# A two-layer encoder: the second attention layer's transposes go from TensorE to VectorE and memory, its loads are split by use, its heads queue in line

## The chip, the cores and the metric

The kernel runs on one core of a Trainium2 chip. The metric is the device time of one execution in microseconds (us), lower is better. Engines are named as in the profile: PE is TensorE (matmuls and transposes), PEld its weight load, DVE VectorE, ACT ScalarE, POOL GpSimd, SP SyncE (it issues loads). ACTq and SPq are the queues in which ACT and SP issue transfers.

## The reference

All tensors are float32; x is 256 tokens by 2048. Cut to what matters here:

```python
for i in range(2):
    hn = rms_norm(h, attn_norm[i])
    # i = 0: windowed attention, 32 heads of 64 in 4 key groups, sink logit
    # i = 1: differential attention, 8 heads of 2 x 128
    h = h + (windowed_gqa_sink, diff_attention)[i](hn, ...)
    h = h + swiglu(rms_norm(h, ffn_norm[i]), w_ffn_in[i], w_ffn_out[i])   # hidden width 5632
    gate = sigmoid(rms_norm(h, ple_gate_norm[i]) @ ple_w_gate[i])
    h = h + rms_norm(p[i] @ ple_w_proj[i], ple_post_norm[i]) * gate

def diff_attention(...):                  # the layer that the change is mostly about
    qkv = h @ w_qkv                       # 2048 x 6144
    q, k = rms_norm(q, q_gain), rms_norm(k, k_gain)    # per head, two maps of 128 each
    sc = q @ k.T * scale - slope * dist   # for each head and each of its two maps
    probs = softmax(sc)
    wts = probs[0] - lam * probs[1]
    o = rms_norm(wts @ v, subln) * (1 - lambda_init)   # 256 columns a head
    return o @ w_o
```

## The kernel before, in words

Every product with a weight matrix is a list of *groups*. A group makes a strip of 512 output columns for all 256 tokens: up to 16 k-tiles of 128 rows, two row tiles of 128 tokens, and three matmuls each (activation low x weight high, high x high, high x low, in a reduced float32 format), so 96 matmuls of width 512 for a full group (L177, `mm<-ws,xt`). There are 9600 of them. The high and low parts of a weight block of two k-tiles come from `split_block`: ACT casts (L139), DVE subtracts (L140). Raw blocks of 1 MB are loaded through SP's queue into three buffers, and split blocks of two k-tiles live in four. `split` and `split_scaled` do the same for activations (ACT L207 or L211, then DVE L208 or L212).

The order in which the code emits instructions is set by `Flow`, a clock that exists only while the program is built. Each wide matmul advances it by `MM = 0.23`; `later(delay, fn)` puts a piece of other work on a heap, and after each matmul at most one step of the earliest due piece is emitted. A piece written as a generator emits one step per `yield` (0.1 on the clock, or the value yielded). If a group needs an operand that isn't there yet, `flow.until` empties the heap ahead of time ("forced"), and the pieces then stand in PE's order back to back. PE follows this order throughout; ACT and DVE follow their written order in the first group only, and are ordered by the compiler's scheduler afterwards.

The matmul contracts over partitions, so activations must be turned before they are used. There are two ways. One is PE transposes of 128x128 through PSUM (L306, L441, L483, L700, L807). The other is `turned`, a *trip through memory*: DVE transposes in blocks of 32x32 (L266), ACT issues one write to DRAM (L268), after 3.0 on the clock four reads that put the blocks in place (L273), and after another 5.0 the consumer's splits. Before, only the feed-forward's hidden values and the residual strips take trips, with a buffer for the write and another for the read.

The stages in order: the first attention layer (`AttentionA`: groups of keys and values, then four of queries), its output projection in parts of 8, 4 and 4 k-tiles, feed-forward and gate, the second attention layer (`AttentionB`), its projection in parts of 8 and 8, feed-forward and gate. The attention pieces are threaded into the groups by `Flow`.

In `AttentionB` a strip of two heads has a group of queries, one of keys, one of values. After a group of queries or keys, `qk_norm` squares (ACT L414), sums (DVE), makes reciprocal roots on POOL (up to L418), and scales the result to `qn` (DVE L430). Then `to_pairs` turns each head by four PE transposes (L441) and splits it. Scores (L449, six matmuls a map) and `exps` (DVE L463 and L466, ACT L469) follow; POOL and DVE combine the two maps, `keys_first` turns the weights by four PE transposes (L483), `weigh` multiplies them with the values (L677, 12 matmuls), the output is normed and `out` turns it by four PE transposes (L700).

In `AttentionA` the same steps run for 16 pairs of heads (scores L449, weights turned at L483, keys at L528, products with values L588). Its buffers are counted in `busy`: a piece whose buffers are taken tries again each 0.6 on the clock (`when`).

At the start x comes in eight pieces of 256 columns, with a weight block behind each second one (`load_x`, `feed.fetch`), and `put_x` turns and splits two pieces at a time.

Of the kernel before, what the change touches and what calls it, by code (L numbers as in the profile page):

```python
# [12 lines left out]
F32 = mybir.dt.float32  # L13
# [72 lines left out]
def encoder(ctx: ExitStack, tc: tile.TileContext, x, p, attn_norm, ffn_norm, a_w_qkv, a_q_norm,  # L86
# [171 lines left out]
    def turned(srcs, then):  # L258


        (tag0, tag1), ap = spare[0], spare[1]
        both = [ap.tile([P, 2, 2, T], F32R, name=t, tag=t, bufs=n).bitcast(F32).rearrange("p a b t -> p (a b t)")
                for t, n in (tag0, tag1)]
        st = both[0].rearrange("p (f t m) -> p f m t", m=NM, t=32)
        for m in range(NM):
            nc.vector.transpose(out=st[:, :, m, :], in_=srcs[m].rearrange("p (f t) -> p f t", t=32))  # L266
        d = dram.tile([P, 2 * W], F32, name="sq32")
        nc.scalar.dma_start(out=d, in_=both[0])  # L268

        def read():  # L270
            for b in range(4):
                r = slice(32 * b, 32 * b + 32)
                nc.scalar.dma_start(out=both[1][r].rearrange("f (k g i) -> f k g i", k=SK, g=4),  # L273
                                  in_=d.rearrange("(g f) (k b i) -> b f k g i", g=4, k=SK, b=4)[b])
            flow.later(5.0, lambda: then(both[1].rearrange("f (k t m) -> f k m t", k=SK, m=NM)))
        flow.later(3.0, read)
# [86 lines left out]
    def put_x(q):  # L363

        if q == 0:
# [31 lines left out]
    spare = [None, None]  # L397

    def phase(name, tags):

        phases.close()
        spare[:] = tags, phases.enter_context(tc.tile_pool(name=name, bufs=1, reuse_waits="tile"))
        return spare[1]
# [72 lines left out]
    busy = {"e": 0, "wT": 0, "q": 0}  # L476
# [12 lines left out]
    def when(kind, limit, take, fn):  # L489

        def piece():
            if busy[kind] + take > limit:
                flow.later(0.6, piece)
            else:
                busy[kind] += take
                return fn()
        return piece

    class AttentionA:
        def __init__(self, norm):  # L500
            self.norm, self.os, self.kd, self.vp = norm, Slots(), [], []
            self.ap = phase("attn0", (("wT", WT_BUFS), ("wT", WT_BUFS)))
# [33 lines left out]
        def queries(self, s):  # L536
            def then(toks):
                for b in range(2):
                    flow.later(5.0 + 8.0 * b, when("q", 2, 1, lambda b=b: self.to_q(2 * s + b, toks, b)))
# [5 lines left out]
        def to_q(self, qg, toks, b):  # L545
# [3 lines left out]
            for i in range(2):  # L549
                flow.later(2.0 + 8.6 * i, when("e", E_BUFS, 2, lambda i=i: self.heads(qg * 2 + i, qT, left)))  # L550

        def heads(self, j, qT, left):
# [8 lines left out]
            if not left:  # L561
                busy["q"] -= 1
# [8 lines left out]
            flow.later(10.0, when("wT", WT_BUFS, 2, lambda: self.turn(j, es)))  # L571

        def turn(self, j, es):
            wts = []
            for e in es:
                yield from keys_first(e, self.ap, WT_BUFS, wts)
                busy["e"] -= 1
            flow.later(3.5, lambda: self.weigh(j, wts))

        def weigh(self, j, wts):  # L580
            ps = at_ps()[:, 0, :]
            n = 0
            for e2 in range(2):
                c0 = j // 4 * P + 64 * (1 - e2)
                for kh in range(2):
                    v, wT = self.vp[kh], wts[e2]
                    for a, b in ((1, 0), (0, 1), (0, 0)):
                        nc.tensor.matmul(ps, v[:, a, c0:c0 + P], wT[:, b, kh, :], start=(n == 0), stop=(n == 11))  # L588
                        n += 1
                        yield  # L590
            busy["wT"] -= 2
# [9 lines left out]
    class AttentionB:  # L601
# [3 lines left out]
        def start(self):  # L605
            self.ap = phase("attn1", (("qk0", 2), ("qk1", 2)))
# [3 lines left out]
        def side(self, s, which):  # L610
# [9 lines left out]
        def turn_side(self, hd, which, toks, b):  # L620
            s = self.hd.setdefault(hd, {"e": {}})
            t = self.ap.tile([P, 2, 2, T], F32R, name=f"qk{which}", tag=f"qk{which}", bufs=2)
# [17 lines left out]
        def scores(self, hd, c):  # L640
# [6 lines left out]
            if c == 1:  # L647
# [8 lines left out]
                flow.later(9.0, lambda: self.turn(hd, e1))  # L656

        def turn(self, hd, e):
            got = []
            yield from keys_first(e, self.ap, 2, got)  # L660
            flow.later(3.5, lambda: self.weigh_when_ready(hd, got[0]))
# [7 lines left out]
        def weigh(self, hd, wT):  # L669
# [16 lines left out]
            def scale():  # L686
                on = []
                for m in range(NM):
                    t = self.ap.tile([P, T], F32, name="on", tag="on", bufs=4)
# [3 lines left out]
                flow.later(2.5, lambda: self.out(hd, on))  # L693
            flow.later(7.0, scale)

        def out(self, hd, on):
            ps = at_ps()
            for j in range(2):
                for m in range(NM):
                    nc.tensor.transpose(ps[:, j, mslice(m)], on[m][:, j * P:(j + 1) * P], ident)  # L700
                    yield
            for j in range(2):
                o = pair()
                split_scaled(o[:, 0, :], o[:, 1, :], ps[:, j, :], subln[:, j:j + 1])
                self.os.put(2 * hd + j, halves_of(o))
# [34 lines left out]
    class FeedForward:  # L740
# [4 lines left out]
        def start(self):  # L745
            self.fp = fp = phase(f"ffn{self.layer}", (("sq32", 2), ("turned", 2)))
# [217 lines left out]
```

## Time and profile before

| | before |
|---|---|
| time, median of 3 runs | 2348.84 us (2347.53 to 2349.82) |
| time of the profiled execution | 2351.27 us |
| its span | 2349.5 us |
| mean granted clock of PE | 0.997 |
| PE busy | 2319.2 us, 99% |
| DVE, ACT, POOL busy | 1383.7, 1118.2, 146.9 us |
| moved by DMA | 459.10 MB |

The median says what a user gets; the durations of single instructions come from the one profiled execution, whose time is 2.43 us above the median. The span runs from its first to its last recorded instruction. A granted clock of 1 stands for 2.4 GHz.

### The profile page before, as it was taken

The page shows a single profiled execution, that of the slowest core. Times are in us where ns is not written, and L with a number is a line of the kernel's source. Part 1 is how long each engine was busy: PE and PEld are TensorE (multiplying, and loading weights), DVE is VectorE, ACT ScalarE, POOL GpSimd, SP SyncE. Part 2 cuts the span into 40 slices and gives each one's busy share as a digit, 9 for nine tenths or more (in the row PEclk, how much of TensorE's full clock was granted, in tenths as well). Part 3 has the DMA queues.
Part 4 walks back from the last instruction along what each step waited for, and adds up shares of the span by engine and source line. Part 5 has one row for each costly group of instructions (what it writes and reads, how often), then busy time and mean ns, then how long its engine had stood idle before and what let it go on. Part 6 is the DMA issues. An engine that isn't in the chain of part 4 may idle for free.

```text
span 2349.5 us, 28062 instructions
## 1 busy us (share of the span) xinstructions
PE 2319.2 (99%) x10525; PEld 1906.5 (81%) x10525; DVE 1383.7 (59%) x1670; ACT 1118.2 (48%) x1557; POOL 146.9 (6%) x311
## 2 busy tenths in 40 slices
PE   8999999999999999999999999999999999999999
PEld 6877778888888888878888888788888888888877
DVE  5777765545554554566666666655545555555564
ACT  5555454444433444455555545554444434444453
POOL 1342000000000000000111120000000000000000
PEclk9999999999999999999999999999999999999999
DMA  6432566556656655577645454766556556655663
GB/s 238 157 112 93 173 231 215 199 197 206 215 187 208 213 196 189 206 235 229 206 160 178 164 177 162 240 235 201 197 193 224 201 189 210 210 197 204 208 218 140
DMA packets 186992, 459.10 MB, mean 195 GB/s; under 512 B 75264, under 2 KB 78440, under 8 KB 186600
## 3 DMA queue, kind: packets, MB, share of 16 engines
q1 hardware_dynamic: 120568, 424.27, 52.1%
q10 hardware_dynamic: 66288, 33.04, 5.2%
q8 instruction: 82, 1.34, 0.2%
q14 instruction: 54, 0.44, 0.1%
HBM read 439.95 MB, written 17.30 MB: 195 GB/s over the span
## 4 chain that ended last, share of the span: by engine, by line
PE 90%; DMA 4%; DVE 2%; ACT 2%; ACTq 1%; issue 1%; POOL 0%; SPq 0%; DVEq 0%
PE mm L177 86%; DMA turned<-sq 2%; PE at L449 1%; PE at L588 1%; DVE ws L140 1%; ACT ws L139 1%; DMA qk<-sq 1%; PE at L483 1%; ACTq L273 1%; PE at L677 1%; DMA raw<-in_a_w_qkv_dram 0%; ACT xt L211 0%; PE at L441 0%; DMA sq<-qk 0%; PE at L807 0%
## 5 line engine op out<-in xcount | busy, mean ns | idle before, releaser
L177 PE MATMUL mm<-ws,xt 128*128 128x512 f32 x9600 | 2286.0, 394 | 12.5 <-DVE ws L140 7.0
L177 PEld LDWEIGHTS mm<-ws,xt 128*128 128x128 f32 x9600 | 1794.6, 188 | 408.7 <-DVE ws L140 13.3
L140 DVE TENSOR_TENSOR ws<-raw,ws 128x1024 fp32r<-128x1024 f32 x800 | 973.1, 1223 | 779.3 <-ACT ws L139 772.5
L139 ACT CAST ws<-raw 128x1024 fp32r<-128x1024 f32 x800 | 837.5, 1052 | 975.0 <-PE mm L177 904.6
L218 POOL TENSOR_SCALAR rs_v<-ssum 128x2 f32<-128x2 f32 x8 | 3.6, 448 | 1690.3 <-DVE ssum L251 1690.3
L335 DVE TENSOR_TENSOR h<-mm,h 128x512 f32<-128x512 f32 x104 | 68.6, 685 | 24.2 <-PE mm L177 24.0
L469 ACT ACTIVATE e<-e,nm 128x257 f32<-128x257 f32 (+1 forms) x96 | 47.9, 501 | 10.1 <-DVE nm L466 9.7
L588 PE MATMUL at<-wT,vp 128*128 128x256 f32 x192 | 49.3, 288 | 0.7 <-DVE wT L208 0.7
L220 POOL TENSOR_TENSOR rs_y<-rs_v,halves 128x2 f32<-128x2 f32 (+2 forms) x29 | 49.0, 1690 | 2.4
L483 PE MATMUL at<-ident,e 128*128 128x128 f32 x160 | 42.2, 272 | 0.7 <-DVE e L463 0.7
L449 PE MATMUL at<-kd,qT 128*128 128x512 f32 x96 | 36.7, 407 | 3.2 <-DVE wT L208 2.5
L779 ACT ACTIVATE silu<-mm,rinv 128x512 f32<-128x512 f32 x44 | 29.9, 688 | 19.1 <-PE mm L177 19.0
L463 DVE SCALAR_TENSOR_TENSOR e<-dist,at 128x256 f32<-128x256 f32 x96 | 36.1, 412 | 2.5 <-PE at L449 2.4
L568 POOL TENSOR_SCALAR e<-e,rd 128x256 f32<-128x256 f32 x64 | 33.1, 532 | 61.7 <-DVE rd L472 61.3
L588 PEld LDWEIGHTS at<-wT,vp 128*128 128x128 f32 x192 | 34.9, 196 | 1.8 <-ACT e L469 1.1
L247 ACT ACTIVATE sq<-h 128x512 f32<-128x512 f32 x48 | 29.9, 624 | 12.9 <-DVE h L335 4.5
L430 DVE TENSOR_TENSOR qn<-mm,rr 128x512 f32<-128x512 f32 x24 | 15.8, 685 | 31.5 <-POOL rr L418 31.5
L211 ACT ACTIVATE xt<-turned,gains 128x256 fp32r<-128x256 f32 x36 | 15.9, 514 | 36.1 <-DMA turned<-sq 36.1
L466 DVE TENSOR_REDUCE nm<-e 128x2 f32<-128x514 f32 (+1 forms) x48 | 32.2, 678 | 0.4
L207 ACT CAST xt<-turned 128x256 fp32r<-128x256 f32 x56 | 19.6, 421 | 24.7 <-DMA turned<-sq 24.7
L208 DVE TENSOR_TENSOR wT<-at,wT 128x512 fp32r<-128x512 f32 x40 | 27.0, 685 | 6.7 <-ACT wT L207 6.6
L787 DVE SCALAR_TENSOR_TENSOR hid<-mm,rinv,silu 128x512 f32<-128x512 f32 x44 | 30.9, 743 | 0.0
(109 smaller groups left out, 719.4 us busy)
## 6 DMA issues: line engine op xcount, KB each, us to landing
raw<-in_w_ffn_in_dram SPq DMA_DIRECT2D x352, 512.0 KB
raw<-in_w_ffn_out_dram SPq DMA_DIRECT2D x176, 512.0 KB
raw<-in_b_w_qkv_dram SPq DMA_DIRECT2D x96, 512.0 KB
raw<-in_ple_w_gate_dram SPq DMA_DIRECT2D x64, 512.0 KB
raw<-in_a_w_qkv_dram SPq DMA_DIRECT2D x40, 512.0 KB
raw<-in_a_w_o_dram SPq DMA_DIRECT2D x32, 512.0 KB
raw<-in_b_w_o_dram SPq DMA_DIRECT2D x32, 512.0 KB
sq<-sq ACTq DMA_DIRECT2D x23, 512.0 KB
```

The costliest lines, as they stand in the source:

```text
L139: nc.scalar.copy(out=ws[:, 0], in_=src)
L140: nc.vector.tensor_tensor(out=ws[:, 1], in0=src, in1=ws[:, 0].bitcast(F32), op=ALU.subtract)
L177: nc.tensor.matmul(ps[m], x[:, a, m], w, start=(k == 0 and i == 0), stop=(k == self.n - 1 and i == 2))
L220: nc.gpsimd.tensor_tensor(out=y, in0=v, in1=halves[:, :n], op=ALU.pow)
L335: nc.vector.tensor_tensor(out=hs, in0=ps[m], in1=hs, op=ALU.add)
L449: nc.tensor.matmul(ps[m], q[:, a, mslice(m)], k[:, b], start=(i == 0), stop=(i == 2))
L463: nc.vector.scalar_tensor_tensor(out=sc[:, m, :T], in0=d[:, m, :], scalar=-slope, in1=pss[m], op0=ALU.mult, op1=ALU.add)
L466: nc.vector.tensor_reduce(out=nm, in_=sc, axis=AX.X, op=ALU.max, negate=True)
L469: nc.scalar.activation(out=sc[:, m, :], in_=sc[:, m, :], func=AF.Exp, bias=nm[:, m:m + 1], accum_out=den[:, m:m + 1])
L483: nc.tensor.transpose(ps[:, kh, mslice(m)], w[:, m, kh * P:(kh + 1) * P], ident)
L568: nc.gpsimd.tensor_scalar(out=e[:, m, :T], in0=e[:, m, :T], scalar1=rd[:, m:m + 1], scalar2=1.0, op0=ALU.mult, op1=ALU.mult)
L588: nc.tensor.matmul(ps, v[:, a, c0:c0 + P], wT[:, b, kh, :], start=(n == 0), stop=(n == 11))
```

## The change

**Trips in the second layer.** Queries, keys, weights and outputs of `AttentionB` are no longer turned by PE. `turned` takes them on a trip, for the whole strip of two heads in the case of queries and keys (512 KB) and for one head in the case of weights and outputs (256 KB, `n=2`). The trip now writes from and reads back into one buffer instead of two.

**Loads by use.** The first weight block is loaded in halves, each behind a piece of x, and `put_x` turns one piece of x at a time with a weight split after each.

**Heads in line.** In `AttentionA` a piece that needs buffers stands in a line (`Budget`) and is started when an earlier piece gives them back, in place of trying again each 0.6; some delays are shorter, and `weigh` emits three matmuls a step.

The diff, cut to its core:

```diff
-        return [(raw, t) for t in range(0, n, 2)]
+        load_rows(raw, w, r0, n, c, slice(0, n))
+        return [(raw, t) for t in range(0, n, 2)]
+
+    def load_rows(raw, w, r0, n, c, t):
         for i in range(2):
-            nc.sync.dma_start(out=raw[:, i, :n, :],
-                              in_=w[2 * c + i, r0 * T:(r0 + n * P) * T].rearrange("(p t n) -> p t n", p=P, t=n))
+            nc.sync.dma_start(out=raw[:, i, t, :],
+                              in_=w[2 * c + i, r0 * T:(r0 + n * P) * T].rearrange("(p t n) -> p t n", p=P, t=n)[:, t])
...
-    def turned(srcs, then):
+    def turned(srcs, then, n=SK):
-        (tag0, tag1), ap = spare[0], spare[1]
-        both = [ap.tile([P, 2, 2, T], F32R, name=t, tag=t, bufs=n).bitcast(F32).rearrange("p a b t -> p (a b t)")
-                for t, n in (tag0, tag1)]
-        st = both[0].rearrange("p (f t m) -> p f m t", m=NM, t=32)
+        tag, bufs, ap = spare
+        both = ap.tile([P, 2, 2, T], F32R, name=tag, tag=tag, bufs=bufs).bitcast(F32)
+        both = both.rearrange("p a b t -> p (a b t)")[:, :n * T]
+        st = both.rearrange("p (f t m) -> p f m t", m=NM, t=32)
         for m in range(NM):
             nc.vector.transpose(out=st[:, :, m, :], in_=srcs[m].rearrange("p (f t) -> p f t", t=32))
-        d = dram.tile([P, 2 * W], F32, name="sq32")
-        nc.scalar.dma_start(out=d, in_=both[0])
+        d = dram.tile([P, n * T], F32, name=f"sq{n}", tag=f"sq{n}")
+        nc.scalar.dma_start(out=d, in_=both)
...
-    def put_x(q):
+    def put_x(i):
...
-        for i in (2 * q, 2 * q + 1):
-            yield from norm_a.turn(2 * i)
-            if i % 2 == 0:
-                feed.split()
+        yield from norm_a.turn(2 * i)
+        feed.split()
...
-    def when(kind, limit, take, fn):
...
+    class Budget:
+        def __init__(self, free):
+            self.free, self.line = free, []
+        def when(self, take, fn):
+            def piece():
+                self.line.append((take, fn))
+                self.serve()
+            return piece
+        def give(self, n):
+            self.free += n
+            self.serve()
+        def serve(self):
+            while self.line and self.line[0][0] <= self.free:
+                take, fn = self.line.pop(0)
+                self.free -= take
+                flow.later(0.0, fn)
...
-            self.ap = phase("attn0", (("wT", WT_BUFS), ("wT", WT_BUFS)))
+            self.qs, self.es, self.wts = Budget(2), Budget(E_BUFS), Budget(WT_BUFS)
+            self.ap = phase("attn0", "wT", WT_BUFS)
...
-                flow.later(2.0 + 8.6 * i, when("e", E_BUFS, 2, lambda i=i: self.heads(qg * 2 + i, qT, left)))
+                flow.later(4.0 + 6.0 * i, self.es.when(2, lambda i=i: self.heads(qg * 2 + i, qT, left)))
...
-            flow.later(10.0, when("wT", WT_BUFS, 2, lambda: self.turn(j, es)))
+            flow.later(8.5, self.wts.when(2, lambda: self.turn(j, es)))
...
-                        yield
+                    yield 0.36
...
-            self.ap = phase("attn1", (("qk0", 2), ("qk1", 2)))
+            self.ap = phase("attn1", "turned", 2)
...
-                for b in range(2):
-                    flow.later(5.0 + 8.0 * b, lambda b=b: self.turn_side(2 * s + b, which, toks, b))
+                turned(toks, lambda xT: self.sides(s, which, xT))
...
-            yield from to_pairs(t, toks, b * T, (gq_b, gk_b)[which])
-            s[which] = t
-            if which == 1:
-                for c in range(2):
-                    flow.later(6.5 + 2.0 * c, lambda c=c: self.scores(hd, c))
+        def sides(self, s, which, xT):
+            for b in range(2):
+                t = self.ap.tile([P, 2, 2, T], F32R, name=f"qk{which}", tag=f"qk{which}", bufs=2)
+                for j in range(2):
+                    x = halves_of(t[:, j])
+                    split_scaled(x[:, 0], x[:, 1], xT[:, 2 * b + j], (gq_b, gk_b)[which])
+                self.hd.setdefault(2 * s + b, {"e": {}})[which] = t
+                if which == 1:
+                    for c in range(2):
+                        flow.later(5.0 + 8.0 * b + 2.0 * c, lambda b=b, c=c: self.scores(2 * s + b, c))
...
-                flow.later(9.0, lambda: self.turn(hd, e1))
+                flow.later(9.0, lambda: turned([e1[:, m, :] for m in range(NM)], lambda xT: self.keys_first(hd, xT), 2))
...
-                    t = self.ap.tile([P, T], F32, name="on", tag="on", bufs=4)
+                    t = self.ap.tile([P, T], F32, name="on", tag="on", bufs=2)
...
-                flow.later(2.5, lambda: self.out(hd, on))
+                turned(on, lambda xT: self.out(hd, xT), 2)
...
-            self.fp = fp = phase(f"ffn{self.layer}", (("sq32", 2), ("turned", 2)))
+            self.fp = fp = phase(f"ffn{self.layer}", "turned", 3)
...
-    for i in range(8):
-        load_x(i)
-        if i % 2 == 1:
-            feed.fetch()
-    feed.fetch()
+    block = feed.todo.pop(0)
+    raw = rawp.tile([P, 2, 4, T], F32, name="raw")
+    for i in range(2):
+        load_x(i)
+        load_rows(raw, *block, slice(2 * i, 2 * i + 2))
+        feed.raw.append((raw, 2 * i))
+    for i in range(2, 8):
+        load_x(i)
+        if i % 2 == 1 and i < 7:
+            feed.fetch()
...
-        for q in range(2):
-            for _ in put_x(q):
-                pass
-        flow.later(6 * MM, lambda: put_x(2))
-        flow.later(24 * MM, lambda: put_x(3))
+        for _ in put_x(0):
+            pass
+        for i in range(1, 8):
+            flow.later(max(2, 14 * i - 24) * MM, lambda i=i: put_x(i))
```

How the order moves is shown at three places. The first is PE's order in the second layer's first strip, in the kernel before: the end of the keys' turning, and the scores of the first head's first map (`qk_9084` are its keys, `qk_8911` its queries).

```order
L177 MATMUL mm<-ws,xt 128x512
L441 MATMUL at<-ident,qn 128x128
L177 MATMUL mm<-ws,xt 128x512 x30
L449 MATMUL at<-qk_9084,qk_8911 128x256 x6
L177 MATMUL mm<-ws,xt 128x512 x2
L441 MATMUL at<-ident,qn 128x128
```

In the changed kernel PE's order at the same scores (`qk_9099` and `qk_9104` are the keys of the strip's two heads) is this:

```order
L309 MATMUL at<-ident,h 128x128
L180 MATMUL mm<-ws,xt 128x512 x255
L450 MATMUL at<-qk_9099,qk_8923 128x256 x6
L180 MATMUL mm<-ws,xt 128x512 x6
L450 MATMUL at<-qk_9099,qk_8923 128x256 x6
L180 MATMUL mm<-ws,xt 128x512 x23
L450 MATMUL at<-qk_9104,qk_8928 128x256 x6
L180 MATMUL mm<-ws,xt 128x512 x6
L450 MATMUL at<-qk_9104,qk_8928 128x256 x6
L180 MATMUL mm<-ws,xt 128x512 x58
```

The transposes at L441 are gone, and wide matmuls alone stand ahead of the scores; the second head's scores come 23 wide matmuls behind the first head's.

The second place is ACT's order in the same strip, from the squares of the keys to the splits of the turned keys. In the kernel before:

```order
L414 ACTIVATE sq<-mm,rinv 128x512
L211 ACTIVATE qk_8964<-at,gq_b 128x2x256
L414 ACTIVATE sq<-mm,rinv 128x512
L139 CAST ws<-raw 128x1024 x6
L211 ACTIVATE qk_9084<-at,cols 128x2x256
L139 CAST ws<-raw 128x1024 x2
```

In the changed kernel:

```order
L415 ACTIVATE sq<-mm,rinv 128x512 x2
L142 CAST ws<-raw 128x1024 x5
L271 DMA sq_9045<-turned 128x1024
L142 CAST ws<-raw 128x1024
L276 DMA turned<-sq_9045 32x16x64 x4
L142 CAST ws<-raw 128x1024 x2
L214 ACTIVATE qk_9099<-turned,cols 128x256 x2
L214 ACTIVATE qk_9104<-turned,cols 128x256 x2
```

Five weight casts stand between the squares and the write of the keys' trip, one between the write and its four reads, and two between the reads and the splits.

The third place is PE's order in the first layer's output projection, after 510 wide matmuls, in the kernel before (pairs of `wT` weights against the values `vp`):

```order
L483 MATMUL at<-ident,e 128x128 x2
L528 MATMUL at<-ident,kn 128x128 x2
L449 MATMUL at<-kd_412,qT 128x512 x6
L588 MATMUL at<-wT,vp_435 128x256 x3
L588 MATMUL at<-wT,vp_439 128x256 x3
...
L588 MATMUL at<-wT,vp_439 128x256 x3
L177 MATMUL mm<-ws,xt 128x512 x6
L483 MATMUL at<-ident,e 128x128
```

In the changed kernel the order there, up to the one piece that is still back to back after 522 wide matmuls, is:

```order
L601 MATMUL at<-wT,vp_441 128x256 x3
L180 MATMUL mm<-ws,xt 128x512
L601 MATMUL at<-wT,vp_437 128x256 x3
L180 MATMUL mm<-ws,xt 128x512
L601 MATMUL at<-wT,vp_441 128x256 x3
L180 MATMUL mm<-ws,xt 128x512 x5
L483 MATMUL at<-ident,e 128x128
L180 MATMUL mm<-ws,xt 128x512
...
L450 MATMUL at<-kd_414,qT 128x512 x3
L442 MATMUL at<-ident,qn 128x128 x4
L483 MATMUL at<-ident,e 128x128 x8
L450 MATMUL at<-kd_414,qT 128x512 x6
L601 MATMUL at<-wT,vp_437 128x256 x3
L601 MATMUL at<-wT,vp_441 128x256 x3
```

Before, two pieces without a wide matmul stand in the projection, the first with scores and 24 products with values; in the changed kernel the first is spread between wide matmuls, and the second remains.

## Rows read from the trace of the kernel before

**Rows 1.** The page: busy time, share of the span and instructions of each engine.

```profile
PE 2319.2 (99%) x10525; PEld 1906.5 (81%) x10525; DVE 1383.7 (59%) x1670; ACT 1118.2 (48%) x1557; POOL 146.9 (6%) x311
```

**Rows 2.** Stages: us, busy PE, PEld, DVE, ACT, POOL (instructions); granted clock, DMA, GB/s.

```profile
160.00:190.00 30.00, 24.57 (x127) 19.08 (x126) 24.43 (x52) 17.73 (x48) 10.71 (x26) 0.94 0.13 45
...
316.00:1130.00 814.00, 812.95 (x3604) 670.34 (x3602) 452.25 (x477) 371.44 (x450) 6.34 (x12) 1.00 0.62 209
1130.00:1480.00 350.00, 350.00 (x1690) 289.52 (x1689) 232.68 (x321) 181.15 (x287) 55.04 (x126) 1.00 0.50 173
1480.00:1530.00 50.00, 48.97 (x217) 39.06 (x216) 35.08 (x49) 28.70 (x49) 4.22 (x6) 1.00 0.82 258
```

**Rows 3.** Lines of PE, 1130 to 1470 us: count | busy us, mean ns | idle before.

```profile
L441 PE MATMUL at<-ident,qn 128*128 128x128 f32 x64 | 17.4, 272 | 0.0
...
L700 PE MATMUL at<-ident,on 128*128 128x128 f32 x32 | 8.7, 272 | 0.0
L483 PE MATMUL at<-ident,e 128*128 128x128 f32 x32 | 8.7, 271 | 0.0
```

**Rows 4.** Timeline of PE, second layer: start us, us, operation, idle before.

```profile
1168.64 13.89 PE L177 MATMUL mm<-ws,xt 128*128 128x512 f32 x60
1182.37 0.27 PE L441 MATMUL at<-ident,qn 128*128 128x128 f32 x1
...
1183.06 0.27 PE L441 MATMUL at<-ident,qn 128*128 128x128 f32 x1
```

**Rows 5.** Timeline of ACT and its DMA queue (ACTq), 1480 to 1530 us.

```profile
1483.04 0.33 ACTq L268 DMA_DIRECT2D sq<-qk  x1
...
1486.53 2.67 ACTq L273 DMA_DIRECT2D qk<-sq  x4
...
1494.38 0.53 ACT L211 ACTIVATE xt<-qk,gains 128x256 fp32r<-128x256 f32 x1 [0.98 <-DMA qk<-sq]
...
1507.18 0.33 ACTq L268 DMA_DIRECT2D sq<-qk  x1
...
1519.82 0.53 ACT L211 ACTIVATE xt<-qk,gains 128x256 fp32r<-128x256 f32 x1 [2.24 <-DMA qk<-sq]
```

**Rows 6.** Timelines of ACT and DVE at the first keys' group's end.

```profile
1168.81 0.69 ACT L414 ACTIVATE sq<-mm,rinv 128x512 f32<-128x512 f32 x1 [1.34 <-PE mm L177]
...
1175.79 0.69 DVE L430 TENSOR_TENSOR qn<-mm,rr 128x512 f32<-128x512 f32 x1 [2.94 <-POOL rr L418]
```

**Rows 7.** Tile sq: duration ns min/median/max, first and last start us.

```profile
L266 DVE STREAM_TRANSPOSE sq<-h x18: 667/686/708, 1001.7 to 2240.6; 128x512 f32<-128x512 f32 x18
```

**Rows 8.** Timelines of PE and DVE, 1335 to 1360 us.

```profile
1343.90 0.88 PE L449 MATMUL at<-qk,qk 128*128 128x256 f32 x6
...
1355.97 1.21 DVE L140 TENSOR_TENSOR ws<-raw,ws 128x1024 fp32r<-128x1024 f32 x1
```

**Rows 9.** Waits of the whole run: us in total, times, longest us.

```profile
ACT xt L211 <- DMA turned<-sq: 36.1, 9, 5.5
...
ACT xt L207 <- DMA turned<-sq: 24.7, 14, 4.6
```

**Rows 10.** Timeline of PE, 150 to 190 us.

```profile
163.78 0.30 PE L483 MATMUL at<-ident,e 128*128 128x128 f32 x1 [0.38 <-DVE e L463]
...
168.75 1.55 PE L449 MATMUL at<-kd,qT 128*128 128x512 f32 x3 [2.52 <-DVE wT L208]
...
174.54 1.91 PE L177 MATMUL mm<-ws,xt 128*128 128x512 f32 x6 [0.46 <-ACT xt L207]
```

**Rows 11.** Timeline of all engines, 0 to 20 us.

```profile
9.79 1.04 ACT L139 CAST ws<-raw 128x1024 fp32r<-128x1024 f32 x1 [3.07 <-DMA raw<-in_a_w_qkv_dram]
...
12.10 2.91 PE L177 MATMUL mm<-ws,xt 128*128 128x512 f32 x6
```

**Rows 12.** The page's DMA queues: packets, MB, share of 16 engines.

```profile
q1 hardware_dynamic: 120568, 424.27, 52.1%
q10 hardware_dynamic: 66288, 33.04, 5.2%
```

More of the change, by code (lines that the diff above doesn't have):

```diff
@@ L272, in read @@
                 r = slice(32 * b, 32 * b + 32)
-                nc.scalar.dma_start(out=both[1][r].rearrange("f (k g i) -> f k g i", k=SK, g=4),
-                                  in_=d.rearrange("(g f) (k b i) -> b f k g i", g=4, k=SK, b=4)[b])
-            flow.later(5.0, lambda: then(both[1].rearrange("f (k t m) -> f k m t", k=SK, m=NM)))
+                nc.scalar.dma_start(out=both[r].rearrange("f (k g i) -> f k g i", k=n, g=4),
+                                    in_=d.rearrange("(g f) (k b i) -> b f k g i", g=4, k=n, b=4)[b])
+            flow.later(5.0, lambda: then(both.rearrange("f (k t m) -> f k m t", k=n, m=NM)))
         flow.later(3.0, read)
@@ L487, in keys_first @@
         into.append(wT)
-    def when(kind, limit, take, fn):
[L491 to L497, printed above, removed]
+    class Budget:
[14 more added lines that the diff above has]
+                flow.later(0.0, fn)
     class AttentionA:
@@ L538, in then @@
                 for b in range(2):
-                    flow.later(5.0 + 8.0 * b, when("q", 2, 1, lambda b=b: self.to_q(2 * s + b, toks, b)))
+                    flow.later(5.0 + 8.0 * b, self.qs.when(1, lambda b=b: self.to_q(2 * s + b, toks, b)))
             def done(ps):
@@ L561, in heads @@
             if not left:
-                busy["q"] -= 1
+                self.qs.give(1)
             es = []
@@ L576, in turn @@
                 yield from keys_first(e, self.ap, WT_BUFS, wts)
-                busy["e"] -= 1
+                self.es.give(1)
             flow.later(3.5, lambda: self.weigh(j, wts))
@@ L589, in weigh @@
                         n += 1
-                        yield
-            busy["wT"] -= 2
+                    yield 0.36
+            self.wts.give(2)
             o = pair()
@@ L655, in scores, with keys_first @@
                                                    in1=e2[:, m, :], op0=ALU.mult, op1=ALU.add)
-                flow.later(9.0, lambda: self.turn(hd, e1))
[L658 to L661, printed above, removed]
+                flow.later(9.0, lambda: turned([e1[:, m, :] for m in range(NM)], lambda xT: self.keys_first(hd, xT), 2))
+        def keys_first(self, hd, xT):
+            wT = self.ap.tile([P, 2, 2, T], F32R, name="wT", tag="wT", bufs=2)
+            for kh in range(2):
+                hi, lo = (wT[:, a, kh].rearrange("p (m t) -> p m t", m=NM) for a in range(2))
+                split(hi, lo, xT[:, kh])
+            flow.later(3.5, lambda: self.weigh_when_ready(hd, wT))
         def weigh_when_ready(self, hd, wT):
@@ L692, in scale, with out @@
                     on.append(t)
-                flow.later(2.5, lambda: self.out(hd, on))
+                turned(on, lambda xT: self.out(hd, xT), 2)
             flow.later(7.0, scale)
-        def out(self, hd, on):
-            ps = at_ps()
+        def out(self, hd, xT):
             for j in range(2):
[L699 to L705, printed above, removed]
+                o = halves_of(pair())
+                split_scaled(o[:, 0], o[:, 1], xT[:, j], subln[:, j:j + 1])
+                self.os.put(2 * hd + j, o)
         def groups(self):
```

14 lines of the change are left out of this document (5 added, 9 removed).

## The prediction

> **What bounds the kernel now.** I read the table of engines first: TensorE (PE) is busy for 2319.2 of 2349.5 us, so time can only come from PE's work or from its idle time [rows 1]. The table by stages says where that idle time is: nothing from 1130 to 1480 us, which is the second attention layer; 5.4 us from 160 to 190, where the first layer's attention runs into its output projection; 1.0 us in 50 from 1480 to 1530 [rows 2]. The list by lines, cut to the second attention layer, gives the work that the change takes from PE there: 64 + 32 + 32 transposes (64 of queries and keys, 32 of outputs, 32 of weights) [rows 3]. The timelines then give what one costs, what PE waits for in the burst, and how long a trip through memory takes.
>
> **The change, part by part.** *PE's transposes.* A row of a transpose lasts 0.27 us [rows 3], but the next matmul starts under it. The starts decide: transposes with a matmul after each begin 0.345 us apart (1182.37, then 1183.06 two on), and 60 matmuls without a transpose take 13.73 us, 0.229 each [rows 4]. A transpose costs 0.345 - 0.229 = 0.116 us, and 128 of them 14.8 us, all of it on the path, since PE does not wait in this stage.
>
> The Trainium skill ("TensorE: Matmul & The Clock Gate", Part 4: PE-mode transpose) says that one takes about 275 ns in a kernel's context. Our row agrees on how long one lasts; by that figure the term would be an estimated 35 us. The spacing of the starts decides against it.
>
> *What takes their place.* Each of 24 trips (8 for queries and keys of 512 KB, 16 for weights and outputs of 256 KB) is VectorE (DVE) transposes, one write and four reads issued by ScalarE (ACT), and splits that wait for the landing. A full one took from the write's issue to the first split 1494.38 - 1483.04 = 11.3 us, and 1519.82 - 1507.18 = 12.6 us [rows 5]. PE no longer waits for its own transposes but may wait for these trips, at three places.
>
> (a) Scores. The keys' group ends at about 1169.4 us (the first square, which waits for the first half alone, starts at 1168.81); the scaled keys start at 1175.79, 6.4 us on [rows 6]. The new order puts both halves (2 x 0.6) and two transposes of 0.69 (2 x 0.65 in a row) [rows 7] behind that: 8.9 us. ACT has five weight casts ahead of the write; at PE's pace (12 matmuls each, 2.75 us) the fifth starts at 11.0. So the write goes out between 8.9 and 11.0, and with the trip and about 1.0 us for a high and a low split the keys are there at 21.2 to 24.6 us. PE comes to the scores 93 matmuls after the group, at 93 x 0.229 = 21.3. The wait is 0 to 3.3 us; I take 1.5, four times: 6 us (0 to 13).
>
> (b) Weights times values. PE starts the second scores of a head at 1343.90. Its exponentials are normed and combined by DVE, the next head's scores begun behind them, and all that DVE now keeps ahead of the transpose ends with the weight split at 1355.97 and its 1.2 us [rows 8]; with the first half of the transpose put between and the second behind, about 0.8 us, the weights can leave at +14.0 us. PE comes for them 87 matmuls and 18 short ones (half the columns, half of 0.229: 0.12 each) on: 19.9 + 2.2 = 22.1. 8.1 us remain. A trip of half the bytes is not in the trace. From below: 3.5 from write to read and 2.7 for the four reads' issue [rows 5], 6.2; from above the full trip, 11.3. I take 8.8, with the 5.2 us behind the last issue halved, and 0.8 for the splits: 9.6, a wait of 1.5 us (0 to 4.0). A second head follows some 8 us later and its trip some 4 us later, so it is mostly covered. Four pairs: 6 us (0 to 18).
>
> (c) Weight casts held up. While ACT issues four reads (4 x 0.65 us) or waits for a landing (36.1 + 24.7 us in 23 trips, 2.6 each) [rows 9], no weight block is cast. Four buffers cover this: a block is cast three blocks ahead (8.2 us), less 2.3 for cast and split, so 5.9 us of delay are free. In the feed-forward stage 1.05 us were lost over 11 trips, in 1480 to 1530 1.03 over 3 [rows 2]: 0.1 to 0.34 a trip, 2 to 8 us for 24. I take 2, since every wait under (a) and (b) gives ACT time to catch up.
>
> The second layer then gains 14.8 and pays 14: about nothing. Its out projection doesn't wait: head 7's output is needed 97 matmuls (22 us) after its last product with values, and a norm of 4 us, a trip and a split come to about 17.
>
> *First layer, heads in line.* PE's order has one forced burst less: before, the products with values of head pairs 5 and 6 stand in one piece after 510 matmuls of width 512 and pair 7's after 522; now only pair 7's are pulled up, at 522. The first burst shows idle of 0.38, 2.52 and 0.46 us [rows 10], 3.4 of the 5.4 us of that window, whose granted clock is 0.94 of 2.4 GHz [rows 2], some 1.8 us more in its 30. Most of that dip follows the 2.52. I take 3.4 + 1.6 = 5 us (3 to 6.5). The second burst stays. The denser heads that follow move about 13 us forward; no place there shows PE waiting today.
>
> *Loads by use.* The first cast waits until 9.79 us for a whole block of 1 MB, loaded behind two pieces of x; the first matmul starts at 12.10 [rows 11]. Half the block behind one piece is half the bytes, so the cast can start when x's splits end, near 7: 2.8 us earlier. The later casts then alternate with x's splits one by one instead of trailing, so I let it stand: 3 us (0 to 4.5).
>
> The feed-forward stages keep one buffer in place of two a trip, with three at hand; trips there are tens of microseconds apart, so I cost this at nothing, up to 1 us if one ever waits.
>
> **The sum.** -14.8 + 14 - 5 - 3 = -8.8 us. The profiled execution took 2351.27 us, of which 2349.5 are its span; it would come to 2342.5. It lies 2.4 above the median of 2348.84, so the forecast is 2340 us, 0.37% less.
>
> **The rivals.** *The trips stay hidden.* If keys land within 21.3 us and weights within 8.1 (the lower ends above), only 2 us are paid: -20.8, 2328 (2324 to 2334). For it: both lower ends lie within reach. Against it: every full trip read took 11.3 us or more.
>
> *The trips eat the gain.* Near the upper ends (a 10, b 13, c 3) the layer pays 26: +3, 2349 with the 8 of the other parts partly lost (2344 to 2353.5). For it: PE has no slack at the scores, by the order itself; the second to fourth strips have outputs' trips in the same queue ahead of the keys'.
>
> *Slower: ACT becomes the bound.* A quarter of the layer is 288 matmuls (66.0 us), 48 short ones (5.8) and 32 transposes (3.7): 75.5 us, 71.8 without the last. ACT is busy for 181.15 of 350 us [rows 2], 39 a quarter. Six trips hold it 0.33 + 2.67 us each for issuing [rows 5] and up to 2.6 for landing [rows 9]: 39 + 33 = 72, just PE's own. From about 6.7 us a trip (79 a quarter) the whole kernel is slower than before by over 0.2%; at 7.5 it is 84, four times 12.2 over 71.8, which against the 22.8 gained gives 2375. For it: landings were waited for up to 5.5 us [rows 9]. Against it: the half trips are shorter, and a cast already running hides part of an issue.
>
> *The memory path is too slow for short pieces.* The Trainium skill ("DMA: Bandwidth & Descriptors", Specifications) wants 512 B at least for line rate; the read-back moves 256 B at a time. Here the queue that carries trips moves 33.04 MB in 5.2% of the engines' time, the weights' queue 424.27 in 52.1% [rows 12]: 22% less per time, not half. 4.2 us of all engines per full trip add 67 us to a layer whose share is 0.50 [rows 2], which makes some 0.75; at twice the price it would be 1.0, weights would come late, and nothing be gained (2352).
>
> **How the numbers follow.** Chances: forecast (2334 to 2344) 0.40, hidden 0.25, eaten 0.24, slower 0.09, short pieces 0.02. I give 2326 to 2352: below it half of the hidden case's best, above it the slower one. The forecast's own range is 2334 to 2346. With 0.2% (4.7 us), about what a measurement of this kernel tells from no change, as the line: faster 0.65, same 0.25, slower 0.10.
>
> **What would show it.** The new profile's PE should hold 128 transposes fewer and 15 us less work. (a) is right if the first score matmul of each strip waits for a split of keys behind a trip, 1 to 2 us, and wrong if it waits for nothing or over 3; (b) the same at the products with values. (c) shows as PE waiting for weight splits in the layer. In 160 to 190 us the 2.5 us wait should be gone and one burst left, and the first large matmul should start near 9.3. What would make me wrong most: a half trip much shorter or longer than 8.8 us, or a burst in the first layer that comes back elsewhere.

## The result and the profile after

The changed kernel takes 2373.76 us (median of 4 runs, 2370.22 to 2376.28) against 2349.33 before: the ratio is 1.0105, interval 1.0092 to 1.0117. It is 24 us slower; the forecast was 2340 us.

The page of the changed kernel, engines and the trips' queue [rows 1, 12]:

```profile
span 2368.4 us, 28116 instructions
...
PE 2313.5 (98%) x10397; PEld 1900.5 (80%) x10397; DVE 1403.8 (59%) x1742; ACT 1117.9 (47%) x1581; POOL 157.0 (7%) x311
...
q10 hardware_dynamic: 104048, 49.82, 8.0%
```

PE has 128 instructions fewer, as it should. But its idle time grew from 2349.5 - 2319.2 = 30.3 us to 2368.4 - 2313.5 = 54.9, and its mean granted clock fell from 0.997 to 0.993, which is 2368.4 x 0.007 - 2349.5 x 0.003 = 9.5 us (the clocks are rounded, so some 2 us either way). So 24.6 + 9.5 - 14.8 = 19.3 us, and the span grew by 18.9: within that rounding the account closes with the term of the transposes as forecast.

The stages of the changed kernel say where [rows 2]:

```profile
160.00:190.00 30.00, 26.58 (x135) 21.01 (x134) 22.80 (x44) 15.29 (x39) 10.16 (x24) 0.94 0.28 97
...
316.00:1130.00 814.00, 812.77 (x3603) 670.40 (x3602) 454.63 (x482) 370.85 (x452) 10.03 (x18) 1.00 0.63 209
1130.00:1480.00 350.00, 319.86 (x1434) 262.05 (x1433) 231.51 (x365) 167.83 (x293) 60.79 (x120) 0.97 0.63 202
```

The second layer, where PE never waited, now has 30.1 us of idle time and a granted clock of 0.97, which is some 10 us more (350 x 0.03). PE's waits in that stage (in total, times, longest) name it:

```profile
PE at L450 <- DVE qk L215: 15.2, 4, 4.8
PE at L693 <- ACT wT L210: 5.5, 4, 1.5
PE mm L180 <- ACT ws L142: 4.6, 3, 1.9
PE mm L180 <- DVE ws L143: 4.4, 6, 1.4
PE at L693 <- DVE wT L211: 0.4, 1, 0.4
```

Scores waited for keys 15.2 us, products with values for weights 5.9, weight splits cost 9.0. PE's timeline in the second strip:

```profile
1224.74 8.78 PE L180 MATMUL mm<-ws,xt 128*128 128x512 f32 x38
1234.83 0.73 PE L180 MATMUL mm<-ws,xt 128*128 128x512 f32 x2 [1.31 <-ACT ws L142]
1236.09 13.89 PE L180 MATMUL mm<-ws,xt 128*128 128x512 f32 x60 [0.53 <-DVE ws L143]
1251.39 7.32 PE L180 MATMUL mm<-ws,xt 128*128 128x512 f32 x31 [1.41 <-DVE ws L143]
1263.40 1.65 PE L450 MATMUL at<-qk,qk 128*128 128x256 f32 x6 [4.70 <-DVE qk L215]
```

The 2 + 60 + 31 = 93 wide matmuls ahead of the scores are the distance that the prediction counted, so the keys' group ends at 1233.5. What ACT does meanwhile:

```profile
1222.38 0.33 ACTq L271 DMA_DIRECT2D sq<-turned  x1
1222.75 1.05 ACT L142 CAST ws<-raw 128x1024 fp32r<-128x1024 f32 x1 [1.19 <-DVE on L706]
1224.95 0.33 ACTq L271 DMA_DIRECT2D sq<-turned  x1
1227.03 6.58 ACTq L276 DMA_DIRECT2D turned<-sq  x8
1233.73 1.99 ACT L142 CAST ws<-raw 128x1024 fp32r<-128x1024 f32 x2 [9.93 <-DMA turned<-sq]
1235.63 1.77 ACT L214 ACTIVATE qk<-turned,gq_b 128x256 fp32r<-128x256 f32 x4
...
1239.09 1.24 ACT L415 ACTIVATE sq<-mm,rinv 128x512 f32<-128x512 f32 x2
...
1250.26 0.33 ACTq L271 DMA_DIRECT2D sq<-turned  x1
...
1253.04 2.63 ACTq L276 DMA_DIRECT2D turned<-sq  x4
...
1262.30 1.78 ACT L214 ACTIVATE qk<-turned,cols 128x256 fp32r<-128x256 f32 x4 [4.52 <-DMA turned<-sq]
```

Two trips fall together, one of queries and one of outputs. ACT issues their eight reads one behind the other and computes nothing for 9.93 us, 6.58 of them for issuing the reads; its first weight cast after that is what PE waits for at 1234.83. The keys' squares start at 1239.09, 5.6 us behind their group. The keys' write leaves 16.7 us behind the group, the first split 12.0 us later. Stretches show the clock around such a wait:

```profile
1263.40:1269.10 5.70, 5.70 (x19) 5.04 (x20) 5.25 (x10) 4.48 (x11) 0.00 (x0) 0.50 0.08 32
```

```profile
1250.00:1260.00 10.00, 7.32 (x31) 5.74 (x31) 6.94 (x8) 4.83 (x6) 0.00 (x0) 1.00 0.93 275
1260.00:1270.00 10.00, 6.60 (x23) 5.78 (x24) 6.69 (x14) 6.31 (x14) 0.00 (x0) 0.66 0.40 145
...
1430.00:1440.00 10.00, 6.11 (x21) 5.40 (x22) 6.24 (x14) 5.98 (x14) 0.00 (x0) 0.66 0.43 155
```

A mean of 0.66 in ten microseconds leaves 3.4 us of full clock out. Part of that falls into the wait: the 5.70 us of work from 1263.40 on ran at the lower of the two levels (1.2 GHz), which costs 2.85 us on top of the 4.7 waited.

### The profile page after: what moved, and what is told of

The parts are those of the page before. It is cut to its first block, busy times and chain, and to the rows that moved or that the text cites. A ratio compares the mean times of both kernels' runs of the same rounds, so it can differ in the third digit from the quotient of the medians.

```text
span 2368.4 us, 28116 instructions
## 1 busy us (share of the span) xinstructions
PE 2313.5 (98%) x10397; PEld 1900.5 (80%) x10397; DVE 1403.8 (59%) x1742; ACT 1117.9 (47%) x1581; POOL 157.0 (7%) x311
## 4 chain that ended last, share of the span: by engine, by line
PE 82%; DMA 8%; ACT 3%; DVE 3%; ACTq 2%; POOL 1%; issue 1%; DVEq 0%; SPq 0%
PE mm L180 79%; DMA turned<-sq 6%; PE at L450 1%; ACTq L276 1%; DMA sq<-turned 1%; ACT ws L142 1%; DVE ws L143 1%; POOL rs_y L223 1%; PE at L601 1%; ACT xt L214 1%; PE at L483 0%; DMA wT<-sq 0%; ACT qk L214 0%; PE at L818 0%; DVE turned L269 0%
## 5 line engine op out<-in xcount | busy, mean ns | idle before, releaser
L180 PEld LDWEIGHTS mm<-ws,xt 128*128 128x128 f32 x9600 | 1799.5, 189 | 416.9 <-DVE ws L143 18.9
L143 DVE TENSOR_TENSOR ws<-raw,ws 128x1024 fp32r<-128x1024 f32 x800 | 972.2, 1222 | 764.5 <-ACT ws L142 753.7
L214 ACT ACTIVATE xt<-turned,gains 128x256 fp32r<-128x256 f32 x48 | 21.3, 514 | 44.7 <-DMA turned<-sq 44.7
L215 DVE SCALAR_TENSOR_TENSOR xt<-turned,gains,xt 128x256 fp32r<-128x256 f32 x48 | 20.8, 485 | 26.9 <-ACT xt L214 26.9
L483 PE MATMUL at<-ident,e 128*128 128x128 f32 x128 | 33.8, 272 | 0.1
L693 PE MATMUL at<-v,wT 128*128 128x256 f32 x96 | 28.0, 292 | 5.9 <-ACT wT L210 5.5
L601 PE MATMUL at<-wT,vp 128*128 128x256 f32 x192 | 32.6, 281 | 0.7 <-DVE wT L211 0.7
L450 PE MATMUL at<-qk,qk 128*128 128x256 f32 x96 | 18.2, 337 | 15.2 <-DVE qk L215 15.2
```

Of the source, the lines that this page charges most:

```text
L143: nc.vector.tensor_tensor(out=ws[:, 1], in0=src, in1=ws[:, 0].bitcast(F32), op=ALU.subtract)
L180: nc.tensor.matmul(ps[m], x[:, a, m], w, start=(k == 0 and i == 0), stop=(k == self.n - 1 and i == 2))
L214: nc.scalar.activation(out=hi, in_=src, func=AF.Copy, scale=scale)
L450: nc.tensor.matmul(ps[m], q[:, a, mslice(m)], k[:, b], start=(i == 0), stop=(i == 2))
L483: nc.tensor.transpose(ps[:, kh, mslice(m)], w[:, m, kh * P:(kh + 1) * P], ident)
```

## The experiments

"Base" is the changed kernel with the second layer turned by PE (the first run). Medians in us; ratios are to the kernel before. The intervals are 4 to 9 us wide, so a difference of 4 us or less between two runs is not clear of them.

| run | what takes trips in the second layer | time | ratio, interval |
|---|---|---|---|
| b_by_pe | nothing (base) | 2339.7 | 0.9961, 0.9946 to 0.9976 |
| start_only / line_only | nothing; one other part alone | 2343.2 / 2342.7 | 0.9975, 0.9966 to 0.9985 / 0.9969, 0.9957 to 0.9980 |
| idle_trips | queries, keys beside PE | 2343.9 | 0.9976, 0.9964 to 0.9987 |
| wo_trips | weights, outputs | 2339.4 | 0.9960, 0.9946 to 0.9974 |
| wo_later | the same, products later | 2335.3 | 0.9938, 0.9924 to 0.9953 |
| qk_trips | queries, keys | 2357.7 | 1.0031, 1.0020 to 1.0042 |
| qk_later | the same, scores later | 2331.0 | 0.9922, 0.9907 to 0.9938 |
| scores_later | all, scores later | 2350.5 | 1.0009, 1.0000 to 1.0018 |
| later_all | all, scores and products later | 2362.4 | 1.0052, 1.0034 to 1.0070 |
| no_o_later | later_all without outputs | 2336.5 | 0.9949, 0.9936 to 0.9963 |
| no_w_later | later_all without weights (products at their old place) | 2352.3 | 1.0016, 1.0007 to 1.0024 |
| sp_issue / later_all_sp | all, issued by SP; the second with both places later | 2415.1 / 2376.7 | 1.0282, 1.0263 to 1.0300 / 1.0119, 1.0101 to 1.0136 |

**Which part.** The first run turns queries, keys, weights and outputs by PE again, and keeps the rest:

```diff
-                turned(toks, lambda xT: self.sides(s, which, xT))
+                for b in range(2):
+                    flow.later(5.0 + 8.0 * b, lambda b=b: self.turn_side(2 * s + b, which, toks, b))
```

> All trips of the second layer are undone: queries, keys, weights and outputs are turned by PE as before; loads by use, heads in line and the one-buffer trips of the feed-forward stay. Theory A (the loss is made by the trips of the second layer alone): the trace after was 9.8 us ahead of before when the second layer began, and it stays ahead: 2339 us, 0.4% under before. Rival B (the other parts cost something that the second layer's trace hides): 2349 or more.

2339.7 us: the other parts gain 9.6, the trips lose 34. The two runs that keep one other part each:

> The kernel before with the loads by use and the one-buffer trips only. The trace after was ahead by 3.1 us when the first group ended, and it stays ahead: 2349.3 - 3 = 2346 us. Rival: the first layer's forced pieces take it back, 2349 us.

> The kernel before with the heads in line and the one-buffer trips only. The trace after gained 6.8 us between the end of the first group and the first feed-forward stage: 2349.3 - 6.5 = 2343 us. Rival: the gain needs the earlier start (the heads' places shift with it), 2347 us or more.

Both are faster than the kernel before by themselves, 5.8 and 6.4 us. Their sum, 12, is a little over the 9.6 of both, within what the intervals allow.

**Which trips.** 

> Only queries and keys take the trip; weights and outputs are turned by PE as before. Theory A (crowding: in strips two to four the outputs' trips meet the queries' trip in ACT's order, ACT is held for 10 us, the keys' squares start 3.9 us late and so the scores wait 4.85 us): without the outputs' trips every strip behaves as the first did, a wait of about 1.2 us, 4 x 1.2 = 5 us, and no drop of the granted clock: 2349 - 9.8 - 7.4 + 5 + 2 = 2339 us. Rival B (the keys' trip itself is too long): scores wait 4 to 5 us in each strip and the clock falls behind them: 2349 - 17.2 + 18 + 8 = 2358 us.

> Only weights and outputs take the trip; queries and keys are turned by PE as before. Theory A (crowding): the two outputs' trips still hold ACT, but no queries' trip stands behind them; products with values wait 1.5 us four times (6), weight splits some 4, the clock stays: 2349 - 9.8 - 7.4 + 10 = 2342 us. Rival B (the keys' trip is the culprit): the same time. Rival C (any trip in this layer costs about what it did, 24 trips gave up 42 us, so 16 of them 28): 2349 - 9.8 - 7.4 + 28 = 2360 us.

Weights and outputs cost nothing net (2339.4 us). Theory A and rival B forecast the same 2342 there, so this run speaks against rival C alone. Queries and keys alone cost 18 us over the base, as rival B had it: theory A's crowding by outputs is not needed for the scores to wait. With queries and keys alone, PE's waits in the layer, and the keys' way in its second strip:

```profile
PE at L450 <- DVE qk L215: 16.5, 4, 7.2
```

```profile
1224.80 29.18 PE L180 MATMUL mm<-ws,xt 128*128 128x512 f32 x128
...
1233.96 1.26 ACT L415 ACTIVATE sq<-mm,rinv 128x512 f32<-128x512 f32 x2
...
1242.39 1.29 DVE L431 TENSOR_TENSOR qn<-mm,rr 128x512 f32<-128x512 f32 x2 [3.22 <-POOL rr L419]
...
1246.06 0.33 ACTq L271 DMA_DIRECT2D sq<-turned  x1
...
1251.82 2.68 ACTq L276 DMA_DIRECT2D turned<-sq  x4
...
1257.07 1.80 ACT L214 ACTIVATE qk<-turned,cols 128x256 fp32r<-128x256 f32 x4 [0.47 <-DMA turned<-sq]
...
1258.49 1.02 PE L450 MATMUL at<-qk,qk 128*128 128x256 f32 x6 [4.51 <-DVE qk L215]
```

From square to scaled keys it takes 8.4 us (7.0 in the first strip before, [rows 6]), a weight split of DVE (1.21 us) stands between them and the transposes, and the reads are issued 5.76 us behind the write. The memory path is nearly full there: a share of 0.96 in the stretch 1246 to 1252, against 0.32 at the queries' write (1218 to 1222), where the reads followed after 2.63 us. Which transfers stood ahead of the write is not shown.

**What a trip costs when nothing waits for it.** The base, with the eight trips of queries and keys beside PE's transposes; the splits of what they bring are left out:

```diff
+                turned(toks, lambda xT: None)
                 for b in range(2):
```

> The kernel with the second layer turned by PE (2339.7 us), and beside it the eight trips of queries and keys, whose values nobody uses: DVE's transposes, the write and the four reads run, the splits of what they bring do not. It prices a trip on which nothing waits. Theory A (PE pays for trips by waiting for what they bring, at a fixed place): 2339 to 2341 us, no wait at weight splits worth naming. Rival B (a trip costs by what it occupies: ACT held while it issues reads, and the memory path): queries and keys by trips cost 18 us over the kernel without them, plus 7.4 saved, so up to 25 us in all; if half of that is occupation, 2352 us.

4.2 us more than the base, about half a microsecond a trip. That is 3 us above theory A's range and far below rival B's 2352; the intervals of the two runs overlap. In its trace PE waits 3.0 us in the layer, all at the transposes of weights for values that DVE has late, and never for a weight split. So what these eight trips occupy is small and the waiting was the price. The run holds no outputs' trips, so it prices no meeting of two.

**Moving the places.** One number, the scores' delay:

```diff
-                        flow.later(5.0 + 8.0 * b + 2.0 * c, lambda b=b, c=c: self.scores(2 * s + b, c))
+                        flow.later(11.0 + 8.0 * b + 2.0 * c, lambda b=b, c=c: self.scores(2 * s + b, c))
```

> The changed kernel with the scores put 6 us later in the order (11.0 in place of 5.0 on the emission clock after the keys' splits), nothing else. Theory A (a wait at a fixed place, 4.85 us or less, and the clock that falls behind it): the waits at the scores (1.2 + 3 x 4.85 = 15.8) and most of the clock's loss (some 8 of 10 us) are gone: 2374 - 24 = 2350 us. Rival B (ACT is the bound of the layer, the wait at the scores only shows it): the wait comes back at the weight splits or the products with values: 2365 us or more.

> Queries and keys by trips, weights and outputs turned by PE, and the scores 6 us later. Theory A (fixed places): without the waits at the scores (1.1, 4.7, 7.3, 4.0) and the clock that fell behind them, only what eight trips occupy is left, 4 us, against 7.4 saved: 2339.7 + 4 - 7.4 = 2336 us. Rival B (the wait moves to the weight splits): 2345 us or more.

Both came out as theory A had it or better: 23 us less with all trips, and with queries and keys alone 27 us less, which makes the fastest kernel of the study. It is 8.7 us below the base, of which the 64 transposes account for 7.4 at the prediction's price; the 4 us of occupation are not found again, and the base has no waits that a later place could save (1.05 us of idle time from 1110 to 1480). In the fastest kernel, PE's waits in the layer, and the stage:

```profile
PE at L483 <- DVE e L668: 0.8, 1, 0.8
```

```profile
1130.00:1480.00 350.00, 349.21 (x1658) 290.70 (x1657) 245.81 (x357) 184.94 (x312) 55.20 (x120) 1.00 0.62 202
```

Then the products with values as well:

```diff
-            flow.later(3.5, lambda: self.weigh_when_ready(hd, wT))
+            flow.later(8.5, lambda: self.weigh_when_ready(hd, wT))
```

> Weights and outputs by trips, queries and keys turned by PE, and the products with values 5 us later behind their weights' splits. The run without the delay came to 2339.4 us, with waits of 1.8 to 2.7 us at the four products with values (8.9 in all) and 64 transposes fewer (7.4). Theory A (fixed places, and these trips hardly hold anything up): the waits go, 2339.4 - 8.9 = 2331 us. Rival B (as in the run with both places later, the wait moves to the weight splits): 2337 us or more.

> Scores 6 us later, as before, and the products with values another 5 us later behind their weights' splits (8.5 in place of 3.5). Theory A (fixed places): the waits at the products with values (some 11 us of 13 in the run with later scores) go too; the weight splits' waits (some 9) stay: 2350.5 - 10 = 2340 us, as fast as with the layer turned by PE. Rival B (the waits move on to the next trip, the outputs', or to buffers): 2348 us or more.

With weights and outputs alone it gains some 4 us of the 9 hoped for, between the two theories (PE now waits 2.8 us for weight splits and 2.3 for outputs at the projection). With all 24 trips it is 12 us slower than with the scores later alone, and rival B holds: against that run the waits at the products are gone (10.8 us), but those for weight splits grew from 5.3 to 14.6 us, so PE's idle time in the stage is no smaller (18.9 us against 17.9). Most of the loss comes behind the stage: the projection waits 8.37 us for the last outputs, whose trip starts later too, and the clock from 1480 to 1520 is 0.87 against 0.98. PE's waits for weight splits in the stage, the wait at the projection, and ACT ahead of the third strip's scores:

```profile
PE mm L180 <- DVE ws L143: 8.0, 9, 2.3
PE mm L180 <- ACT ws L142: 6.6, 4, 2.6
```

```profile
1485.35 5.16 PE L180 MATMUL mm<-ws,xt 128*128 128x512 f32 x11 [8.37 <-ACT xt L214]
```

```profile
1323.21 2.77 ACTq L276 DMA_DIRECT2D turned<-sq  x4
1326.18 0.46 ACTq L271 DMA_DIRECT2D sq<-turned  x1
1326.74 2.00 ACT L142 CAST ws<-raw 128x1024 fp32r<-128x1024 f32 x2 [6.28 <-DVE turned L269]
1332.33 2.63 ACTq L276 DMA_DIRECT2D turned<-sq  x4
1335.06 0.94 ACT L214 ACTIVATE xt<-turned,subln 128x256 fp32r<-128x256 f32 x2 [6.32 <-DMA raw<-in_b_w_qkv_dram]
```

ACT computes 2 us in 12: reads of outputs, the keys' write, the keys' reads each hold the casts behind them. Two runs leave out one kind of trip:

> The kernel with scores and products with values later (2362.4 us), but outputs turned by PE: 16 trips, of queries, keys and weights. Theory A (the outputs' trips meet those of the next strip's queries and keys in ACT's order, and ACT's weight casts stand behind both): without them no wait at weight splits, about as with queries and keys alone, 2331 us, less up to 3.7 for 32 more transposes saved: 2328 to 2333 us. Rival B (24 trips are too many for ACT, whichever they are; two thirds give up two thirds): 2345 us or more.

> The same with weights turned by PE in place of outputs: 16 trips, of queries, keys and outputs, scores later. Theory A (outputs' trips meet those of queries and keys): most of the loss of the run with 24 trips stays, 2350 us or more. Rival B (the number of trips): as the other run, 2345 us; rival C (neither pair meets when the weights' trips are gone): 2328 to 2335 us.

Sixteen trips without outputs come to 2336.5, sixteen with outputs and without weights to 2352.3. All of PE's waits in the layer without outputs' trips, and its waits for weight splits without weights' trips:

```profile
PE at L716 <- DVE on L706: 6.5, 3, 2.6
```

```profile
PE mm L180 <- DVE ws L143: 11.1, 6, 3.7
PE mm L180 <- ACT ws L142: 2.8, 3, 1.5
```

Without outputs' trips no weight split is waited for; with them the splits cost 13.9 us, about as much as with all 24 trips. So it isn't the number: it is outputs' trips beside those of queries and keys. Nor is it the memory path, which is fuller in the faster run (0.67 against 0.64 from 1130 to 1440). That ACT's order is what can't take them is read from the trace above. Theory A holds, though the first run is 3 us above its range: PE's transposes of outputs wait 6.5 us for DVE.

**Another queue.** In `turned`, `nc.scalar.dma_start` becomes `nc.sync.dma_start`, in the changed kernel and in the one with both places later:

> The changed kernel with the writes and reads of all trips issued by SP, in whose queue the weight loads stand, in place of ACT. Theory A (in the second layer ACT is held for up to 10 us while it issues reads behind a write, so weight casts, the keys' squares and with them the scores are late): the waits at weight splits (11 us) go, the scores wait about 1 to 2 us each: 2374 - 11 - 11 - 5 of clock = 2347 us. Rival B (SP's order holds trips behind loads that wait for a free buffer, up to one block, 5.5 us): keys come 3 to 5 us later still and weight loads are held too: 2385 us or more.

> Both: later scores and products with values, and trips issued by SP. Theory A for both: no wait at the places, none at weight splits: 2340 - 9 = 2331 us, faster than either kernel. Rival B (SP's order): 2345 us or more, with PE waiting for weights behind loads that SP issued late.

Both are slower than the same kernel with ACT issuing (2373.8 and 2362.4), in time as rival B had it. The queue in the first of them, at the second strip's keys:

```profile
1273.97 0.40 SPq L271 DMA_DIRECT2D sq<-turned  x1
1276.27 1.12 SPq L135 DMA_DIRECT2D raw<-in_b_w_qkv_dram  x2
1281.82 2.60 SPq L276 DMA_DIRECT2D turned<-sq  x4
...
1288.46 1.65 PE L450 MATMUL at<-qk,qk 128*128 128x256 f32 x6 [7.62 <-DVE qk L215]
```

The reads leave 7.85 us behind the write, with two loads between; 4.3 us of that SP waits for the write to land. In the second run, PE's waits at the scores and for weight splits:

```profile
PE at L450 <- DVE qk L215: 27.7, 4, 9.7
PE mm L180 <- DVE ws L143: 0.4, 1, 0.4
PE mm L180 <- ACT ws L142: 0.3, 1, 0.3
```

With ACT free of the trips the weight splits cost PE 0.7 us in place of 14.6, which fits that ACT's order held the casts. It does not settle it: the keys come later still, the scores wait 27.7 us though they stand 6 us later, and such waits give the casts time as well. In the first run the splits still cost 8.4 us (9.0 with ACT issuing); there ACT's casts wait 25.4 us for blocks that load late. In the second run PE waits for keys, and not for weights as rival B had it.

## Why the prediction was wrong

- **Transposes, -14.8: right.** 128 instructions are gone, and the account closes with that number to some 2 us.
- **(a) Scores, 6 us (0 to 13): the step that failed most.** 15.2 us. The first strip waited 1.1, as forecast; the second to fourth 4.7 to 4.8. The step priced the first strip and took it four times. In the later ones the two trips that meet ahead of the keys make the squares 5.6 us late, so the write left 16.7 us behind the group (forecast 8.9 to 11.0). The meeting is one cause of two: with queries and keys alone the squares were only some 1.3 us late (the 128 matmuls end at 1253.98, and 93 x 0.229 before that is 1232.7), but the write left 12.1 us behind them, its reads were held for 5.76 us, and the scores still waited 4.51. The trip itself, 12.0 us from write to first split in the changed kernel and 11.0 there, was priced right. The prediction named the outputs' trips in the same queue, but only as what speaks for a rival, without a price.
- **(b) Products with values, 6 us (0 to 18): right**, 5.9.
- **(c) Weight casts, 2 us (2 to 8): mis-sized.** 9.0. The step reckoned with trips one by one, each under the 5.9 us that the buffers cover. Two together held ACT for 9.93.
- **The clock: a term that was missing.** The sum has no term for it in the layer, where it costs some 10 us. Moving the scores took 12.2 us of idle time out of it (350 - 332.07 is left) and 23 us of the whole.
- **Heads in line -5, loads by use -3: right in sum, in part by luck.** The base gains 9.6. Loads by use alone gain 5.8, above their range of 0 to 4.5; the first matmul starts at 7.74 us and not 9.3 (12.10 before). Heads in line alone gain 6.4, but not where the forecast put it: the 2.52 us wait of [rows 10] is gone, yet from 160 to 190 us the idle time fell by 2.0 us and not by 3.4, and the clock stayed at 0.94. Where the rest comes from is not shown.
- **The rival "ACT becomes the bound"** gave 2375 us, near the measured 2373.8, at a chance of 0.09. The number is luck, the mechanism half right. ACT is not short of time (167.83 of 350 us busy): with the scores moved, the same 24 trips cost 23 us less. But it is held in its order, and once the places are moved that is much of what remains. Short pieces did not decide it: with queries and keys alone 8 full trips read at 256 B and the kernel is the fastest. (The share of the memory path in the layer is 0.63; the prediction's 0.75 should be 0.69 by its own terms, 0.50 + 67 / 350.)
- **Range and chances.** The case "the trips eat the gain" let the layer pay 26 us, which by its own terms makes 2352 us and not 2349; the layer paid 30.1 of waits and some 10 of clock, and the projection behind it 4.3 where it was 1.0 (70 us each, from 1490 and from 1480).

## What to carry to other kernels

Work taken from a full engine gains only if the results still come by the place where that engine takes them: price the whole way (chain, write, read, splits) in the steady state and not in the first round, and move the consumer with it; here one delay was worth 27 us. Transfers that ACT issued here held its arithmetic behind them, for the issue (6.58 us for eight reads) and while a read waited for its write to land, so look for the two that meet, not at their mean. A wait can cost more than its length: behind the 4.70 us wait shown, TensorE worked for 5.70 us at half its clock.

## What was unexpected

The granted clock after a wait: behind the 4.7 us waits of the second and fourth strip it was 0.66 over ten microseconds, behind the first strip's 1.1 us (1180 to 1190) it stayed 1.00, and in 160 to 190 us it is 0.94 in both kernels though the 2.52 us wait is gone. Nor does that wait alone make the dip: with loads by use alone (start_only) it stands there too, and the clock of the stretch is 1.00. And with queries and keys alone, a write of 512 KB held its reads for 2.63 us with the memory path at 0.32, and for 5.76 with it at 0.96; in the fastest kernel it is the queries' write that holds them, 5.41 us at 0.81. The share alone doesn't set it.
